# Two-block hybrid layer: first norm's small steps on VectorE, loads of the start reordered, and the small slots kept open through the end of the second block

## The chip, the cores and the metric

One core of a Trainium2 chip runs the whole program. The metric is the device time of one execution in microseconds; the span in a profile runs from the first to the last instruction of the core.

## The reference, cut to what matters

One sequence of 1024 positions and width 1024 passes two blocks, in float32.

```
h = rms_norm(x) @ w_in;  x += [rg_lru(conv(lru_x)) * gelu(lru_gate), sc_b * conv(sc_c * sc_x)] @ w_out
u = conv(rms_norm(x) @ w_up);  x = rms_norm(x + (gelu(gate) * up) @ w_down)        # end of the first block
h = x @ w_in_2  ->  x_q (512), x_kv (256), k_rope (64), gate_a (512), u_pool (512), gate_b (512)
q = rms_norm(x_q) @ w_uq;  k_nope, v = rms_norm(x_kv) @ w_ukv;  rotary parts turned by position
y_a = softmax(causal(q k^T) * scale) v * silu(gate_a)                              # 4 heads
y_b = pool(u_pool, windows 2, 4, 8, 16) * silu(gate_b)
x = layer_norm(alpha * x + [y_a, y_b] @ w_out_2)
```

## The kernel before, in words

Every float32 product is made of three float32r products: an operand is cut into a high part (a cast on ScalarE) and a low part (a subtraction on VectorE), and high x high, high x low and low x high are summed in PSUM. A matmul takes 128 x 128 weights and 512 columns.

**Pairs.** A projection from 1024 inputs is made for two groups of 128 outputs at a time (`Pair`, L229), as seven products of half depth in the manner of Strassen instead of eight. A pair's weight sums are made by loads that accumulate onto a tile in SBUF (`G.dma_start(..., accum_op=ADD)`, L251, L252, L267), issued from GpSimd. `prep_hi` and `prep_lo` (L260, L265) cut an operand, `product` (L269) runs twelve matmuls into one of three PSUM banks of the pair ("x", "y", "z"; the table `GROUP`), and `evac` adds the bank into two result tiles. `Pairs.step` runs one product, keeps the cuts five products ahead and the loads two pairs ahead. The first two pairs of each `Pairs` are interleaved and have `apart` set: their second product has a bank of its own.

**Due times.** `later(d, fn)` puts work off by `d` products; `tick` runs what is due. So the small work of a finished pair (recurrence, convolution, pooling) is spread over the products of the next. The source order sets the priority of the instructions, and a scheduler may change their order on an engine where one is not ready in its model. SyncE (SP) issues the plain loads and stores in one queue, GpSimd (POOL) the accumulating ones and some stores.

**The start.** `start` (L1021) loads x tiles 0 and 1, the gain, x tiles 2 and 3, all pieces of the first two pairs, x tiles 4 to 7, eleven pieces of small vectors (`vec_load`, L148) and the gate weights (`gate_weights_load`, two clears on GpSimd and four loads). `transition` (L472) then norms the eight tiles: `Norm.a` squares and sums (ScalarE), takes the root and the reciprocal (VectorE, L404); `Norm.b` makes five steps on a column of 128 x 1 (GpSimd, L412 to L416) and scales the tile (VectorE, L418); `Norm.T` transposes it on TensorE and cuts it into the moving operands `Hop`.

**The stages.** Fourteen pairs of the mixer with the recurrence (`lru_pair`), its output product (`Rows`), 24 pairs of the feed-forward, its output product, and nine pairs of the second block (`second`, L909): the pooled groups 3 to 0, the low-rank keys and queries, the attention gates. In the middle of these `kr_product` makes the rotary keys.

**End of the second block.** Small tiles of 128 x 1024 float32 come from one pool "u" of `NU` = 23 slots (`U`, L73). After the last pair all due work is drained and the pools are closed and opened anew, the small one with `NU_LATE` = 35 slots, the larger PSUM tiles with two banks each (`PS`). Then come, in this order: `pooled_rows` (fetch pooled rows and weights, L1080; cut, L1133, L1134; product "wob"; row sums with the residual, L1148; store), `q_rope` and `q_nope` for two halves of the heads, `masks_make`, `keys_values`, and attention, in a branch that runs when positions are in order. `head_load` (L1391) fetches the five tiles of the next head (QN, KN, QT) at the second of a head's eight steps; the rotary tiles come by `rot_load`, the turned keys by `keys_rope`.

## Time and profile before

| | us |
|---|---|
| median of 3 runs | 1782.14 |
| lowest and highest | 1781.0, 1783.39 |
| the profiled execution's own time | 1776.74 |
| its span | 1774.6 |

The profile is of one execution, 5.4 us faster than the median. Engines: PE is TensorE's matmuls, PEld its weight loads, DVE is VectorE, ACT ScalarE, POOL GpSimd, SP SyncE. The mean granted TensorE clock of the span is 0.973 of full speed. An engine's idle time is put down to the instruction that, by the profile, ended last among those it waited for; that is inferred, and a wait can bear the name of an instruction that only stood next to the true cause. L110 is the line of every product.

### The profile page before, as it was taken

To read this page: it belongs to the slowest core of one execution; us is meant where nothing else is said; L and a number is where in the kernel's file an instruction comes from. 1 tells how busy PE (TensorE), PEld (TensorE's weight loads), DVE (VectorE), ACT (ScalarE), POOL (GpSimd) and SP (SyncE) were. 2 spreads that over 40 slices of the span, in tenths; PEclk is the share of its full clock that TensorE was granted. 3 is DMA by queue.
4 is the path that set the end of the run, shared out by engine and by line. 5 is a ranking of instruction groups with operands and counts; after the bars stand their busy time and mean duration, and the time that the engine had idled before them with its cause. 6 is when DMAs were issued, how large, how long until landed. Compare 5 with 4: busy or idle time off the path is not lost. (4 is left out here: it accounts for less than half of the span.)

```text
span 1774.6 us, 20249 instructions
## 1 busy us (share of the span) xinstructions
PE 1635.7 (92%) x7347; PEld 1339.8 (75%) x7347; DVE 1191.5 (67%) x1711; ACT 778.3 (44%) x1147; POOL 371.6 (21%) x387
## 2 busy tenths in 40 slices
PE   3898999899998999999999999999999997678997
PEld 3676777678886887887888888888777786557885
DVE  3868666776498797767666754455985755456777
ACT  4566556753064444444444411121653433026761
POOL 4224243211032322222231000010231200020016
PEclk7999999999999999999999999999999998889998
DMA  8556586197156978777774852420586728746232
GB/s 212 103 105 131 105 157 119 30 332 194 14 142 111 191 143 167 150 147 145 160 142 107 306 204 95 101 42 18 150 167 128 149 54 320 217 145 230 99 116 109
DMA packets 272814, 255.36 MB, mean 144 GB/s; under 512 B 18398, under 2 KB 238404, under 8 KB 272708
## 3 DMA queue, kind: packets, MB, share of 16 engines
q1 hardware_dynamic: 168244, 186.80, 32.6%
q0 software_dynamic: 103744, 65.03, 25.4%
q10 hardware_dynamic: 720, 2.18, 0.4%
q8 instruction: 60, 0.98, 0.2%
q14 instruction: 46, 0.38, 0.1%
HBM read 199.56 MB, written 52.82 MB: 142 GB/s over the span
## 5 line engine op out<-in xcount | busy, mean ns | idle before, releaser
L110 PE MATMUL o<-yw 128*128 128x512 f32 x1632 | 375.9, 390 | 0.0
L110 PEld LDWEIGHTS o<-yw 128*128 128x128 f32 x1632 | 305.5, 188 | 63.7 <-DVE yw L530 0.8
L570 DVE TENSOR_TENSOR x<-x,o 128x512 f32<-128x512 f32 x160 | 108.6, 684 | 135.3 <-PE o L110 135.1
L529 ACT CAST yw<-yraw 128x1024 fp32r<-128x1024 f32 x34 | 35.8, 1052 | 193.9 <-PE o L110 172.3
L110 PE MATMUL wob<-yw 128*128 128x512 f32 x192 | 47.0, 408 | 9.0 <-DVE yw L1134 8.9
L402 ACT ACTIVATE xn<-x 128x1024 f32<-128x1024 f32 x24 | 25.6, 1068 | 60.4 <-DVE x L570 54.0
L110 PEld LDWEIGHTS wob<-yw 128*128 128x128 f32 x192 | 37.9, 199 | 18.1 <-ACT yw L1133 9.3
L530 DVE TENSOR_TENSOR yw<-yraw,yw 128x1024 fp32r<-128x1024 f32 x34 | 41.6, 1222 | 14.9 <-ACT yw L529 14.7
L431 PE MATMUL T<-cst,xn 128*128 128x128 f32 x128 | 19.4, 308 | 27.4 <-DVE xn L418 23.1
L530 DVE TENSOR_TENSOR yw<-wraw,yw 128x1024 fp32r<-128x1024 f32 x34 | 41.4, 1218 | 0.4 <-ACT yw L529 0.4
L1459 POOL TENSOR_TENSOR rt<-rt,lng 128x1024 f32<-128x1024 f32 x6 | 14.4, 2403 | 125.3 <-ACT rt L1458 125.3
L431 PEld LDWEIGHTS T<-cst,xn 128*128 128x128 f32 x128 | 17.1, 160 | 30.1 <-DVE xn L418 19.5
L760 DVE TENSOR_TENSOR ffc<-ffc,ffc 128x1024 f32<-128x1024 f32 x24 | 29.4, 1224 | 13.2 <-ACT ffc L757 13.1
L529 ACT CAST yw<-wraw 128x1024 fp32r<-128x1024 f32 x34 | 35.7, 1051 | 3.1 <-DMA wraw<-in_w_down_dram 2.4
L251 POOL DMA_DIRECT2D wu3s<-in_w_in_dram x1 | 1.3, 1282 | 167.9 <-DVE x L570 167.9
L757 ACT ACTIVATE ffc<-ffc 128x1024 f32<-128x1024 f32 x24 | 25.5, 1061 | 24.9 <-DVE ffc L754 24.9
L412 POOL TENSOR_SCALAR ss<-ss 128x1 f32<-128x1 f32 x24 | 7.4, 309 | 132.8 <-ACT ss L403 132.1
L110 PE MATMUL o<-PT,Vh 128*128 128x256 f32 x160 | 30.2, 286 | 4.0 <-DVE PT L1366 3.4
L1345 ACT ACTIVATE sc<-sc,st 128x256 f32<-128x256 f32 (+3 forms) x32 | 26.3, 823 | 15.2 <-DVE st L1344 15.1
L110 PEld LDWEIGHTS o<-PT,Vh 128*128 128x128 f32 x160 | 25.3, 191 | 5.8 <-DVE PT L1366 4.2
L662 POOL TENSOR_TENSOR i<-i,xc 128x1024 f32<-128x1024 f32 x8 | 20.7, 2590 | 42.3 <-ACT i L661 42.3
L437 ACT CAST B<-T 128x512 fp32r<-128x512 f32 x36 | 20.4, 593 | 20.0 <-PE T L431 19.9
(1365 smaller groups left out, 4442.0 us busy)
## 6 DMA issues: line engine op xcount, KB each, us to landing
GY<-ffc SPq DMA_DIRECT2D x24, 512.0 KB
yraw<-GY SPq DMA_DIRECT2D x24, 512.0 KB
wraw<-in_w_down_dram SPq DMA_DIRECT2D x24, 512.0 KB
x<-in_x_dram SPq DMA_DIRECT2D x16, 512.0 KB
yraw<-Y SPq DMA_DIRECT2D x12, 512.0 KB
wraw<-in_w_out_dram SPq DMA_DIRECT2D x12, 512.0 KB
Y<-i SPq DMA_DIRECT2D x8, 512.0 KB
R<-x SPq DMA_DIRECT2D x8, 512.0 KB
```

What stands on the lines that cost most here:

```text
L110: PE.matmul(ps, lhsT=l, rhs=r, start=(first and j == 0), stop=(last and j == n - 1), skip_group_check=not first)
L402: A.activation(xn, X[t], AF.Square, accum_out=ss[:, 0:1])
L431: PE.transpose(ps[:, k * P:(k + 1) * P], src[:, c * P:(c + 1) * P], ident)
L437: A.copy(Hop[m][:, 0, :, sl], src)
L529: A.copy(s[:, j], src)
L530: V.tensor_tensor(s[:, j + 1], src, f(s[:, j]), SUB)
L570: V.tensor_tensor(X[t][:, ns], X[t][:, ns], ps, ADD)
L662: G.tensor_tensor(i, i, st.pop("xc"), MUL)
L757: A.activation(st["g"], st["g"], AF.Gelu_apprx_tanh)
L760: V.tensor_tensor(st["u"], st["u"], st["g"], MUL)
L1345: A.activation(s, s, AF.Exp, scale=QK_SCALE, bias=st[:, 1:2], accum_out=st[:, 2:3])
L1459: G.tensor_tensor(r, r, gB, MUL)
```

## The change

- The first norm's five small steps run on VectorE (`Norm(gB, False, None, V)`); the other norms keep GpSimd.
- The first operand of the first two pairs (`load_first`) is loaded ahead of x tiles 4 to 7, the rest of these pairs behind them; the small vectors and the gate weights are loaded behind the transition.
- The product of number 3 of the first two pairs of every `Pairs` has a bank of its own, no longer the one of number 5; the saved copy of number 5 is added on VectorE after number 6.
- In the recurrence the exponential, its square and the multiplication follow the hyperbolic tangent one tick later, and the rest moves by a tick.
- The rotary key weights are cut at a due time of 14 products and no longer inside `kr_product`. In `second` the pair of pooled group 0 changes place with the first gate pair.
- The pool "u" stays open with 23 slots until the end, and a pool "v" with 12 slots takes the place of the pool "b" for tiles of attention that live long (rotary tiles, turned keys, head 0, masks, first output weights).
- The pooled fetch of groups 3 and 2 and the cut of group 3 stand four products before the end of the pairs; the pooled rows then run in the old pools, with the groups in the order 3, 2, 1, 0, one PSUM bank for each half row, two row sums of half width instead of one, and the first half of the query weights fetched and cut among them. The low-rank keys, the rotary tiles and the second half of the query weights follow after the pools are changed; the masks come behind the last query product.

```
-NU_LATE = 35
+NU_LATE = 12
+    def UV(nm, dt=F32, shape=(P, 1024)):
+        return pools["v"].tile(list(shape), dt, name=f"{nm}_{count[0]}", tag="V", bufs=NU_LATE)
...
+        def load_first(self):
+            if self.a is None:
+                self.a = U(self.nm + "a", F32, (P, 2, 4, P))
+                SY.dma_start(self.a.rearrange("p h k c -> p (h k) c"),
+                             self.ap[:, self.cols[0]:self.cols[0] + P].rearrange("(k p) c -> p k c", p=P))
...
-            new = m in FIRST or m == 2 and self.apart
+            new = m in FIRST or m in (2, 3) and self.apart
...
                 V.tensor_tensor(za[:, n1], (za[:, n1] if 3 in self.seen else zb[:, n0]), ps, SUB)
+                if self.apart:
+                    V.tensor_tensor(za[:, n1], za[:, n1], self.m5, ADD)
...
-            later(10, lru_2)
-            later(11, lru_3)
-            later(12, lru_4)
-            later(13, lru_5)
+            later(9, lru_2)
+            later(10, lru_2b)
+            later(12, lru_3)
+            later(13, lru_4)
+            later(14, lru_5)
...
-                    ga_pair(0), pool_pair(0), ga_pair(2)])
+                    pool_pair(0), ga_pair(0), ga_pair(2)])
...
-        mix.load(2)
+        for p in mix.pairs[:2]:
+            p.load_first()
         for t in range(4, NT):
             X[t] = U(f"x{t}")
             SY.dma_start(X[t], I["x"][0, t * P:(t + 1) * P, :])
-        vec_load()
-        gate_weights_load()
-        norm = Norm(gB, False, None)
+        mix.load(2)
+        norm = Norm(gB, False, None, V)
...
         transition(norm, mix, lambda t: mix.prep(min(max(t - 3, 0), 4)))
+        vec_load()
+        gate_weights_load()
...
-    second.run(lambda: None, lambda: kr_product(kr["raw"]))
-    drain()
-    for nm in ("p", "b", "h", "u"):
-        close_pool(nm)
-    sizes["U"] = NU_LATE
-    open_pool("u")
...
+    later(14, lambda: kr.update(w=split(kr["raw"], "wkr", (P, 8, P))))
...
+    def pooled_begin():
+        pooled_fetch(3)
+        pooled_fetch(2)
+        pooled_cut(3, True)
...
+        pooled_fetch(1)
+        pooled_fetch(0)
+        inv.append(fetch("linv", LINV_d[0]))
...
+        wq["r0"], wq["n0"] = q_rope_load(0), q_nope_load(0)
+        ps = [[PB("wob"), PB("wob")] for _ in range(4)]
+        for e in POOLED:
+            if e < 3:
+                pooled_cut(e)
             for t in range(4):
                 for n in range(2):
-                    products(ps[t][ri], three(y[e], w[e], li, ri), e == 0, True)
+                    products(ps[t][n], terms(e, t, n), e == 3, True)
...
         for t in range(4):
+            rx[t] = fetch("rx", R2_d[t])
+        for t in range(2):
             out(t, ps[t])
         low_norm(LQ, inv[0], 76, "lq")
+        for t in range(2, 4):
+            out(t, ps[t])
+        q_rope_cut(0)
+        q_nope_cut(0)
...
-    pooled_rows()
-    raws = [q_rope_load(0), q_nope_load(0)]
-    q_rope(0, raws[0])
-    raws += [q_rope_load(1), q_nope_load(1)]
+    second.run(pooled_begin, lambda: kr_product(kr["w"]))
+    pooled_rows()
+    for nm in ("p", "b", "h"):
+        close_pool(nm)
+    open_pool("v")
+    open_pool("h")
+    open_pool("p", PSUM)
+    wq["r1"], wq["n1"] = q_rope_load(1), q_nope_load(1)
+    rot_load()
...
+    q_rope(0)
     tick()
-    q_nope(0, raws[1])
-    wkv_raw = [fetch("wkv", w_ukv[k * P:(k + 1) * P, :]) for k in range(2)]
-    q_rope(1, raws[2])
+    q_nope(0)
+    q_rope_cut(1)
+    q_nope_cut(1)
+    wkv = [fetch("wkv", w_ukv[k * P:(k + 1) * P, :]) for k in range(2)]
+    keys_rope()
+    q_rope(1)
+    low_norm(LKV, inv[1], 80, "lkv")
     tick()
+    for k in range(2):
+        wkv[k] = split(wkv[k], "wkv")
+    q_nope(1)
+    LQ.clear()
     masks_make()
-    q_nope(1, raws[3])
-    LQ.clear()
     keys_values()
```

## Rows read from the trace of the kernel before

**Rows 1.** The page's first part: busy time, share of the span and number of instructions of each engine.

```profile
PE 1635.7 (92%) x7347; PEld 1339.8 (75%) x7347; DVE 1191.5 (67%) x1711; ACT 778.3 (44%) x1147; POOL 371.6 (21%) x387
```

**Rows 2.** The table of stretches. Columns: stretch (us from the start of the span), its length, busy us (and instructions) of PE, PEld, DVE, ACT and POOL, granted TensorE clock, busy share of the DMA engines, GB/s moved.

```profile
0.00:26.70 26.70, 6.79 (x37) 6.60 (x37) 2.42 (x11) 6.82 (x14) 11.55 (x30) 0.75 1.05 298
26.70:42.90 16.20, 8.83 (x48) 8.02 (x49) 13.17 (x19) 13.21 (x28) 5.06 (x13) 0.71 0.57 89
1465.30:1474.40 9.10, 0.18 (x2) 0.00 (x1) 1.93 (x3) 3.15 (x3) 0.00 (x0) 0.79 0.85 312
1474.40:1521.50 47.10, 47.03 (x192) 37.87 (x192) 31.20 (x26) 12.61 (x12) 0.00 (x0) 0.93 0.87 307
...
1533.20:1541.60 8.40, 8.39 (x24) 6.30 (x24) 0.68 (x1) 0.00 (x0) 0.00 (x0) 0.66 0.66 201
1465.30:1614.60 149.30, 113.47 (x444) 89.40 (x444) 80.84 (x94) 37.88 (x39) 17.93 (x31) 0.86 0.72 240
```

**Rows 3.** TensorE's waits from 0 to 96 us: who waited for whom, us in total, times, longest.

```profile
PE T L431 <- DVE xn L418: 23.1, 4, 18.8
PE wl L110 <- ACT wl0m L303: 4.7, 1, 4.7
```

**Rows 4.** The order of time from 0 to 75 us, all engines. Columns: start us, duration us, engine, line, operation, tiles written and read, shapes, count, and in brackets the engine's idle time before it and what ended it.

```profile
7.22 0.35 DVE L404 RECIPROCAL ss<-ss 128x1 f32<-128x1 f32 x2 [5.95 <-ACT ss L403]
...
13.26 1.50 POOL L251 DMA_DIRECT2D wl0s<-in_w_in_dram  x1 [12.80 <-DMA wl0s<-in_w_in_dram]
...
19.41 2.79 POOL L613 MEMSET gates<- 128x1024 f32 x2
...
22.31 0.99 POOL L412 TENSOR_SCALAR ss<-ss 128x1 f32<-128x1 f32 x4
...
25.36 3.67 DVE L418 SCALAR_TENSOR_TENSOR xn<-x,ss,g 128x1024 f32<-128x1024 f32 x3 [13.37 <-POOL ss L416]
...
42.91 5.04 PE L110 MATMUL wl<-B,wl0op 128*128 128x512 f32 x12
```

**Rows 5.** TensorE's waits from 1465 to 1615 us: us in total, times, longest.

```profile
PE qr L110 <- ACT wqrh L103: 13.4, 2, 11.7
PE wob L110 <- DVE yw L1134: 8.9, 1, 8.9
```

**Rows 6.** The order of time of TensorE's and SyncE's (SPq) instructions from 1440 to 1545 us, columns as in the fourth group.

```profile
1453.08 8.32 PE L110 MATMUL wga<-T,wga2op 128*128 128x512 f32 x36
...
1467.47 0.34 SPq L1080 DMA_DIRECT2D yb<-YB  x1
...
1526.57 1.47 SPq L1168 DMA_DIRECT2D wqr<-in_w_uq_dram  x2
...
1533.80 0.63 PE L110 MATMUL qr<-lql,wqrh 128*128 128x512 f32 x1
1534.23 0.63 PE L110 MATMUL qr<-lqh,wqrl 128*128 128x512 f32 x1
```

**Rows 7.** The small column tiles "ss" of the norm from 0 to 60 us: count, shortest, median and longest in ns, first and last start.

```profile
L404 DVE RECIPROCAL ss<-ss x8: 154/164/166, 7.2 to 48.6; 128x1 f32<-128x1 f32 x8
...
L413 POOL TENSOR_TENSOR ss<-ss x8: 187/193/715, 23.4 to 48.9; 128x1 f32<-128x1 f32 x8
```

**Rows 8.** The table of stretches again, 5 us each, at the start; columns as in the second group.

```profile
5.00:10.00 5.00, 2.85 (x20) 2.66 (x18) 0.33 (x2) 3.26 (x8) 0.00 (x0) 1.00 1.02 360
10.00:15.00 5.00, 0.00 (x0) 0.00 (x0) 0.33 (x2) 1.61 (x5) 1.74 (x2) 0.82 1.21 298
```

**Rows 9.** DMA issues from 0 to 60 us: count, size of one, median us from issue to landing.

```profile
wl0s<-in_w_in_dram POOLq DMA_DIRECT2D x4, 256.0 KB, 6.4
```

**Rows 10.** The order of time from 1262 to 1300 us (first two pairs of the second block), columns as in the fourth group.

```profile
1276.00 0.62 ACT L260 CAST wu3op<-wu3s 128x512 fp32r<-128x512 f32 x1 [2.09 <-DMA wu3s<-in_w_in_dram]
...
1278.38 0.68 DVE L265 TENSOR_TENSOR wu3op<-wu3s,wu3op 128x512 fp32r<-128x512 f32 x1
...
1279.05 4.61 PE L110 MATMUL wu<-B,wu3op 128*128 128x512 f32 x12 [3.01 <-ACT wu3m L303]
```

**Rows 11.** TensorE's waits from 95 to 365 us (the mixer).

```profile
PE ws L110 <- ACT ws2z L289: 3.1, 1, 3.1
```

**Rows 12.** The order of time from 1330 to 1365 us, around the rotary key product, columns as in the fourth group.

```profile
1344.18 1.14 ACT L260 CAST wqop<-wqs 128x512 fp32r<-128x512 f32 x2 [6.30 <-DMA wqs<-in_w_in_dram]
...
1345.44 0.68 DVE L300 TENSOR_TENSOR wu2z<-wu2z,wu 128x512 f32<-128x512 f32 x1
...
1346.27 4.17 PE L110 MATMUL wu<-B,wu2op 128*128 128x512 f32 x12 [3.45 <-ACT wkrh L103]
```

**Rows 13.** Groups of VectorE's instructions from 1465.3 to 1617 us: line, operation, tiles, shapes, count, busy us, mean ns of one, idle before them and what ended it.

```profile
L1148 DVE SCALAR_TENSOR_TENSOR rx<-rx,wob 128x1024 f32<-128x1024 f32 x8 | 9.8, 1220 | 18.5 <-DMA rx<-Q 11.4 <-PE wob L110 7.0
...
L1280 DVE SCALAR_TENSOR_TENSOR mtmp<-lk,qf,mtmp 128x256 f32<-128x256 f32 x8 | 3.8, 483 | 0.2
```

**Rows 14.** All DMA traffic from 1465.3 to 1614.6 us.

```profile
DMA packets 14971, 35.84 MB, mean 240 GB/s; under 512 B 4571, under 2 KB 6619, under 8 KB 14966
```

**Rows 15.** The chain of work that ended last, one piece: start us, us, what.

```profile
1497.33 5.81 DMA rx<-Q
```

**Rows 16.** SyncE's issues from 1650 to 1710 us, in attention: the fetch for the last head, and of the residual rows for the last product.

```profile
1657.06 0.33 SPq L1395 DMA_DIRECT2D kn<-KN  x1
...
1707.55 0.32 SPq L1424 DMA_DIRECT2D rt<-RR  x1
```

More of the change, by code (lines that the diff above doesn't have):

```diff
@@ L69 @@
     count = [0]
-    sizes = {"U": NU}
     def U(nm, dt=F32, shape=(P, 1024)):
         count[0] += 1
-        return pools["u"].tile(list(shape), dt, name=f"{nm}_{count[0]}", tag="U", bufs=sizes["U"])
+        return pools["u"].tile(list(shape), dt, name=f"{nm}_{count[0]}", tag="U", bufs=NU)
+    def UV(nm, dt=F32, shape=(P, 1024)):
+        count[0] += 1
+        return pools["v"].tile(list(shape), dt, name=f"{nm}_{count[0]}", tag="V", bufs=NU_LATE)
     def HT(nm, dt=F32R, shape=(P, 8, 512)):
@@ L1116, in keys_rope @@
             SY.dma_start(b[32 * r:32 * r + 32, :], KR_d[32 * o:32 * o + 32, :])
-        later(2, lambda: KR.update(w=split(rotate_2(a, b), "kk")))
-    def pooled_rows():
-        y, w, rx = [], [], {}
-        for e in range(4):
-            y.append(fetch("yb", YB_d[e]))
-            w.append(fetch("wob", w_out2[512 + e * P:512 + (e + 1) * P, :]))
-        inv = [fetch("linv", LINV_d[0])]
+        later(2, lambda: KR.update(w=split(rotate_2(a, b), "kk", of=UV)))
+    py, pw, rx, inv, wq = {}, {}, {}, [], {}
@@ new lines, in pooled_fetch, with pooled_cut @@
+    def pooled_fetch(e):
+        assert id(YB_d[e]) in stored
+        py[e] = fetch("yb", YB_d[e])
+        pw[e] = fetch("wob", w_out2[512 + e * P:512 + (e + 1) * P, :])
+    def pooled_cut(e, small=False):
+        if small:
+            py[e], pw[e] = split(py[e], "yb"), split(pw[e], "wob")
+            return
+        s = HT("yw", F32R, (P, 4, 1024))
+        for j, src in ((0, py[e]), (2, pw[e])):
+            A.copy(s[:, j], src)
+            V.tensor_tensor(s[:, j + 1], src, f(s[:, j]), SUB)
+        py[e], pw[e] = (s[:, 0], s[:, 1]), (s[:, 2], s[:, 3])
@@ new lines, with out, terms @@
+    POOLED = (3, 2, 1, 0)
+    def pooled_begin():
+        pooled_fetch(3)
+        pooled_fetch(2)
+        pooled_cut(3, True)
+    def pooled_rows():
+        def out(t, ps):
+            r = rx.pop(t)
+            for n in range(2):
+                ns = slice(n * 512, (n + 1) * 512)
+                V.scalar_tensor_tensor(r[:, ns], r[:, ns], ALPHA, ps[n], MUL, ADD)
+            SY.dma_start(R3_d[t], r)
+        def terms(e, t, n):
+            return three(py[e], pw[e], (slice(None), slice(t * P, (t + 1) * P)),
+                         (slice(None), slice(n * 512, (n + 1) * 512)))
+        pooled_fetch(1)
+        pooled_fetch(0)
+        inv.append(fetch("linv", LINV_d[0]))
+        assert id(LINV_d[0]) in stored
@@ L1156, in pooled_rows @@
-        later(1, rot_load)
-        later(3, keys_rope)
+        for t in range(2, 4):
+            out(t, ps[t])
+        q_rope_cut(0)
+        q_nope_cut(0)
         for t in range(4, NT):
-            p = PS("wob")
-            mm_rows(p, y, w, t)
-            out(t, p)
+            rx[t] = fetch("rx", R2_d[t])
+            ps = [PB("wob"), PB("wob")]
+            for n in range(2):
+                products(ps[n], [x for e in POOLED for x in terms(e, t, n)])
+            out(t, ps)
             tick()
@@ L1196, in q_nope_load, with q_nope @@
         return raw
[L1198 to L1199 removed]
+    def q_nope(p):
+        w = wq.pop(f"n{p}")
         for j in range(2):
@@ L1296, in masks_make @@
         V.tensor_copy(in_order, below[:, 3:4])
-        a, b, c = (U("mask", BF16, (P, 2, S)) for _ in range(3))
+        a, b, c = (UV("mask", BF16, (P, 2, S)) for _ in range(3))
         G.memset(a[:, :, 0:768], 0.0)
@@ L1494 @@
         attention(False)
-    for nm in ("h", "u", "p"):
+    for nm in ("h", "v", "u", "p"):
         close_pool(nm)
```

77 lines of the change are left out of this document (31 added, 46 removed).

## The prediction

> **What bounds the kernel now.** I read the page first: TensorE is busy 92% of the span [rows 1], so time can only come out of the stretches in which it waits or runs at its lower clock. The table of stretches shows where these are [rows 2]. In the first 26.7 us TensorE works 6.79 us, and from 1465.3 to 1614.6, between the last pair of the second block and attention, it is busy 113.47 of 149.3 us at a granted clock of 0.86. The other stages leave little.
>
> For the start I went to TensorE's waits and then to the order of time. It waits 18.8 us for the first normalised tile [rows 3]. VectorE had the first reciprocals at 7.22 us, but the five small steps behind them stand on GpSimd's queue, which first waits until 13.26 for a load that it is to accumulate onto, then clears the gate tiles at 19.41, and comes to the steps at 22.31; the first scaled tile follows at 25.36 and the first product of a pair at 42.91 [rows 4].
>
> For the second block I read the waits of that stretch: 13.4 us (11.7 of it once) for the cut of the rotary query weights and 8.9 us for the first pooled operand [rows 5]. Both are late because their loads are: the pooled fetch is issued at 1467.47, after the pairs have ended, and the query weights at 1526.57, behind all the row stores on SP's queue [rows 6].
>
> **The change, part by part.** *Start.* Forty small steps go from GpSimd to VectorE. One costs 0.19 us on GpSimd, and VectorE's reciprocal of the same column 0.16 us [rows 7]: 40 x 0.16 = 6.4 us more on VectorE, of which five steps (0.8 us) stand ahead of the first tile, so that it can be scaled at about 8 us and not at 25.4, 17 us sooner. GpSimd's queue keeps its accumulating loads and holds nothing up with them. Then the loads decide. Up to the last tile of x there are now 11 transfers of 0.52 MB (x, gain, two first operands), 5.8 MB, at the 298 to 360 GB/s of the crowded windows [rows 8]: 16 to 19 us, so landing at 19 to 22. The six pieces of the two pairs that were loaded before these tiles now follow them (1.6 MB, 4 to 5 us), and a sum lands 6.4 us after its issue [rows 9], at about 30. ScalarE, in order, may have to wait there with tiles still to cut. If nothing of that bites, the start gains 16; if the first product comes no earlier and VectorE's added steps count (it was busy 13.17 of the 16.2 us before that product [rows 2]), it loses 2. I take **-10**, a little above the middle, because the pause that is removed lies ahead of everything else. Eleven small vector loads, two clears and four gate loads move behind the normalisation; they are wanted only when the first pair is complete, so nothing, and 3 us if a slot makes them late.
>
> *Own bank for the fourth product of the first two pairs.* In the second block TensorE waits 3.0 us at that product and the profile names the copy out of its bank [rows 10]. But the operand of the same product was cast only at 1276.00, after ScalarE had waited for its accumulating load, and its low part is done at 1279.06: the product would have stood there anyway. In the mixer the same wait is 4.7 us [rows 3]. The price is six more VectorE adds of 0.68 us [rows 10]. I take **0**, between -4 (the mixer's wait) and +4 (the adds).
>
> *The recurrence's steps spread by one tick.* The same instructions, so no busy time; TensorE's waits on ScalarE's copies, such as 3.1 us once [rows 11], may get shorter: **-1**, between -5 and +3.
>
> *Cut of the key-rotary weights, made earlier.* The wait of 3.45 us in front of that product bears the cut's name, but ScalarE came to it only after 6.30 us of waiting for another pair's load, and VectorE's subtraction at 1345.44, which the product needs, was behind the same [rows 12]: **0**, or -3.5 at best. The swapped order of two pairs: nothing, the same work.
>
> *Second block's end.* The pools of small slots are no longer closed, so the fetch and first cut of the pooled rows stand four products ahead of the end, the fetches of the query operands at its end, and the rotary weights are cut while the pooled product runs. From 1465.3 to the last value product there are 432 matmuls; 36 of them in one run take 8.32 us, (8.32 - 0.39)/35 = 0.227 us each [rows 6], so 98 us is TensorE's own part of the 149.3. Of the other 51 us TensorE is idle for 36 (149.3 less 113.5 [rows 2]); 15 go into matmuls 0.43 us apart, as at 1533.80 and 1534.23 after a pause [rows 6], where the granted clock averages 0.66 [rows 2], between the levels of 1.2 and 2.4 GHz. What is late next? VectorE has 80.84 us there [rows 2], and two half instructions for each row sum cost a little more than the one of 1.22 [rows 13], some 2 us: 83 of 98, no bound but dense. The transfers are nearer: 35.84 MB [rows 14], of which 2 MB move ahead of the stretch; at the 307 to 312 GB/s of its crowded parts [rows 2] the rest takes 109 us, though the next head's loads in it can slip. I take 110 us for the stretch, **-39**, because that bound is the nearest; the ends are 101 (TensorE alone and 3 us of evacuations, -48) and 134 (waits and half clock return to two thirds, -15).
>
> The Trainium skill, page DMA: Bandwidth & Descriptors, section "Anatomy of one DMA — SWDGE (gpsimd) path", puts the moving part of a transfer at bytes over 436 GB/s. By it the 33.8 MB would take an estimated 78 us, under TensorE's 98, and the stretch would be 101; this trace's crowded parts, at 307 to 312 GB/s [rows 2], do not reach that.
>
> *Masks and attention.* The mask steps now come behind the last query product. Eight steps of 0.48 us are the largest of their kind [rows 13]; VectorE may end them after TensorE has ended the values. In attention 23 shared slots and 12 of a second kind replace 35 shared: **+3**, between 0 and +12.
>
> **Sum**: -10 + 0 - 1 + 0 - 39 + 3 = -47. The profiled execution took 1776.74 us, so 1730; the median of the runs, 1782.14, lies 5.4 higher, so **1735**. All best ends give -77, all worst +9, with 3 for late gates. A measurement here can tell about 0.2%, 3.6 us, from no change.
>
> **Rivals.** *TensorE alone bounds the end and the start gains all*: -16 - 1 - 48 + 1 = -64, 1718. For it: VectorE is under 98 us. Against: the transfers' crowding. By the rate on the Trainium skill's page DMA: Bandwidth & Descriptors it would be so.
>
> *The waits come back as others*: 125 us for the stretch, because the row tiles (5.81 us from issue to landing [rows 15]) or VectorE's queue are late where the weights were: -10 - 1 - 24 + 3 = -32, 1750. For it: VectorE already sat waiting 11.4 us for those tiles [rows 13].
>
> *The order of the source is not the order of issue.* GpSimd's clear of the gate tiles stands ahead of the accumulations in the source and ran after them [rows 4]; if the loads come in an order of their own, the start keeps only what the small steps give, -3: -40, 1742.
>
> *Slower: slots.* Where more than 23 of the shared small tiles are alive, a head's five tiles can be fetched only when the former head's last scores have freed theirs. Then three head changes cost a fetch each, 5 x 0.52 MB at the 240 GB/s of the mean [rows 14], 11 us, where the trace fetches them well ahead, at 1657.06; the four last loads, at 1707.55 [rows 16], another 9; and the last four row tiles of the pooled product two landings of 5.81: 33 + 9 + 12 = 54, net +7, 1789. It decides from 19 tiles alive at a head's fetch. I count 16 (five of the current head, four score tiles, one gate, four outputs, two weights) and 21 with the fetch, so it should not bite; later, at the last head, 28 are wanted for a few steps, which is in my +3.
>
> **Chances.** Forecast 0.56 (own range 1720 to 1752), TensorE alone 0.15, waits return 0.17, order of issue 0.05, slots 0.07. The range 1712 to 1766 leaves out the slower case and the far ends. Faster 0.91, same 0.02, slower 0.07.
>
> **What would show it.** Start: first scaled tile near 8 us, first pair product between 26 and 35. Bank: the copy's name gone from TensorE's waits, another in its place. End: pooled product beginning within 1 us of the last pair's, no wait above 3 us for query weights, some 110 us to the first scores, clock near 1. Attention: SP fetching a head's tiles as early as now. I am wrong if the first product stays behind 38 us, or if TensorE still waits over 25 us in that stretch.

## The result, and the profile after

The changed kernel takes 1729.28 us (median of 4 runs, 1726.95 to 1730.28), the kernel before 1781.57 beside it: ratio 0.9703, 95% interval 0.9687 to 0.9720. 1735 was forecast, 1712 to 1766 as the range. The profiled execution took 1726.95, with a span of 1725.2 against 1774.6, so 49.4 us are to be found in the trace.

TensorE's busy time hardly moves [rows 1]; as the span is shorter, its share rises. VectorE has 54 instructions more (the 40 small steps, six adds of number 5, eight more row sums at half width), GpSimd 40 fewer. The page of the profile, first part:

```profile
PE 1627.0 (94%) x7347; PEld 1334.4 (77%) x7347; DVE 1195.2 (69%) x1765; ACT 777.0 (45%) x1147; POOL 359.4 (21%) x347
```

The table of stretches, cut at the landmarks that answer to [rows 2] (first transposes 9.48, first pair product 34.19, last pair's end 1445.4, first scores 1559.4). Columns: stretch, length, busy time of PE, PEld, DVE, ACT, POOL, granted clock, DMA share, GB/s.

```profile
0.00:9.50 9.50, 6.60 (x37) 6.41 (x37) 2.80 (x18) 4.46 (x9) 0.20 (x4) 1.00 0.77 277
9.50:34.20 24.70, 9.03 (x49) 7.42 (x49) 16.98 (x46) 18.07 (x40) 7.98 (x6) 0.63 1.14 255
34.20:95.00 60.80, 57.56 (x254) 46.03 (x253) 56.06 (x109) 33.33 (x57) 16.12 (x13) 0.98 0.70 125
...
1445.00:1488.70 43.70, 43.70 (x194) 36.22 (x193) 24.97 (x29) 9.36 (x10) 0.00 (x0) 1.00 0.68 230
1488.70:1520.00 31.30, 23.14 (x92) 18.19 (x92) 12.65 (x12) 5.35 (x6) 5.21 (x10) 0.84 0.73 210
1520.00:1559.60 39.60, 36.31 (x154) 29.29 (x153) 31.09 (x41) 15.69 (x17) 12.02 (x20) 0.96 0.64 200
1445.00:1559.60 114.60, 103.15 (x437) 83.69 (x436) 68.71 (x81) 30.41 (x33) 17.23 (x30) 0.94 0.68 214
1559.60:1725.00 165.40, 141.11 (x832) 122.78 (x830) 121.08 (x308) 94.52 (x167) 32.55 (x16) 0.94 0.38 137
```

The pooled product (first row of the second group) now runs without a gap. The stretch from the last pair to the first scores is 114.6 us, was 149.3 (147.9 if it too is ended at its first scores, at 1613.2); TensorE stands for 11.4 of it, most between 1488.7 and 1520. From the first scores to the end it is 165.8, was 161.4.

The start in order of time (it answers to [rows 4]; rows of the engines' timelines put in one order):

```profile
8.14 1.28 DVE L428 SCALAR_TENSOR_TENSOR xn<-x,ss,g 128x1024 f32<-128x1024 f32 x1
9.48 1.09 PE L441 MATMUL T<-cst,xn 128*128 128x128 f32 x8 [1.84 <-DVE xn L428]
...
20.45 1.48 POOL L258 DMA_DIRECT2D wl0s<-in_w_in_dram  x1 [20.00 <-DMA wl0s<-in_w_in_dram]
...
25.88 0.62 ACT L267 CAST wl0op<-wl0s 128x512 fp32r<-128x512 f32 x1 [5.25 <-DMA wl0s<-in_w_in_dram]
26.53 0.69 DVE L272 TENSOR_TENSOR wl0op<-wl0s,wl0op 128x512 fp32r<-128x512 f32 x1 [6.01 <-ACT wl0op L267]
...
29.42 1.94 PE L441 MATMUL T<-cst,xn 128*128 128x128 f32 x8 [9.53 <-DVE ss L422]
...
34.19 2.06 PE L112 MATMUL wl<-B,wl0op 128*128 128x512 f32 x4
```

The pause of [rows 4] is gone, and another has come: ScalarE, in order, stands 5.25 us for the accumulated sum of the first pair, VectorE and TensorE behind it. TensorE's waits from 1440 to 1580 (us in total, times, longest), beside [rows 5]:

```profile
PE qr L112 <- ACT wqrh L105: 7.8, 1, 7.8
PE t L1398 <- ACT sc L1388: 6.1, 1, 6.1
PE kn L112 <- DVE knl L106: 3.2, 1, 3.2
```

The wait for the pooled operand (8.9 us) is gone; the one for the query weights is now at the second half of the heads.

### The profile page after: what moved, and what is told of

Its sections match the earlier page's. It is cut to its first block, busy times and chain, and to the rows that moved or that the text cites. A ratio compares the mean times of both kernels' runs of the same rounds, so it can differ in the third digit from the quotient of the medians.

```text
span 1725.2 us, 20241 instructions
## 1 busy us (share of the span) xinstructions
PE 1627.0 (94%) x7347; PEld 1334.4 (77%) x7347; DVE 1195.2 (69%) x1765; ACT 777.0 (45%) x1147; POOL 359.4 (21%) x347
## 5 line engine op out<-in xcount | busy, mean ns | idle before, releaser
L540 DVE TENSOR_TENSOR yw<-yraw,yw 128x1024 fp32r<-128x1024 f32 x34 | 41.5, 1221 | 14.9 <-ACT yw L539 14.8
L112 PE MATMUL wob<-yw 128*128 128x512 f32 x144 | 34.1, 389 | 0.0
L112 PEld LDWEIGHTS wob<-yw 128*128 128x128 f32 x144 | 27.0, 188 | 5.6
L1380 DVE CUSTOM_DVE_ANT_0 sc<-s,mask 128x256 f32<-128x256 f32 (+3 forms) x32 | 25.9, 819 | 6.3 <-PE s L112 5.8
L1398 PE MATMUL t<-cst,sc 128*128 128x128 f32 x160 | 23.3, 277 | 6.6 <-ACT sc L1388 6.1
```

The lines of the kernel that those rows point to most:

```text
L112: PE.matmul(ps, lhsT=l, rhs=r, start=(first and j == 0), stop=(last and j == n - 1), skip_group_check=not first)
L540: V.tensor_tensor(s[:, j + 1], src, f(s[:, j]), SUB)
L1380: V.tensor_tensor_reduce(s, ps[:, 0:w], masks[causal][i][:, 0:w], 1.0, -3.0e38, ADD, MAX, st[:, 0:1])
L1398: PE.transpose(ps[:, k * P:(k + 1) * P], s[:, k * P:(k + 1) * P], ident)
```

## A table of landmarks

The program issues the same products in the same order in all kernels (but for the places named), so the first matmul of a pair is a landmark. Times of the changed kernel's profiled execution in us, and how much later (+) or earlier (-) each other kernel's is there:

| | first pair | mixer's output | 2nd block, first pair | group 2 | group 1 | last gate | first scores | span |
|---|---|---|---|---|---|---|---|---|
| after | 34.2 | 361.6 | 1238.4 | 1309.2 | 1362.1 | 1426.2 | 1559.4 | 1725.2 |
| before | +8.7 | +16.0 | +18.0 | +14.9 | +19.8 | +18.7 | +53.8 | +49.4 |
| v_steps_alone | +1.4 | +4.7 | +7.9 | +6.2 | +12.3 | +11.0 | +45.8 | +41.6 |
| steps_gpsimd | +13.4 | +22.4 | +21.4 | +18.2 | +17.6 | +18.0 | +19.1 | +19.5 |
| loads_old | +1.5 | +7.1 | +5.0 | +2.6 | +2.3 | +2.3 | +3.8 | +4.2 |
| prep_order | -5.0 | +1.1 | +5.0 | +5.2 | +5.0 | +5.1 | +5.8 | +5.8 |
| bank_shared | +0.7 | +4.9 | +12.4 | +10.0 | +10.4 | +10.7 | +10.3 | +10.3 |
| lru_kr_old | -0.5 | +1.2 | +0.8 | -2.5 | +5.7 | +5.7 | +5.6 | +5.6 |
| masks_early | -0.1 | +0.7 | -1.2 | -4.2 | -4.4 | -4.3 | +1.2 | -6.3 |
| q1_cut_early | +0.1 | +3.4 | +2.4 | -0.7 | -1.0 | -1.0 | 0.0 | -0.1 |
| fetch_late | +0.6 | +3.9 | +2.3 | -0.2 | -0.7 | -0.7 | -1.2 | -1.0 |
| queries_late | -0.5 | -0.8 | -2.6 | -5.3 | -5.7 | -5.5 | -5.2 | -5.1 |
| cuts_masks_early | +0.3 | +1.9 | +2.3 | +1.0 | +0.5 | +0.6 | +3.5 | -4.0 |
| groups_forward | +0.5 | +3.1 | +1.8 | -1.2 | -1.5 | -2.8 | +9.4 | +9.8 |

The last six rows are edited only behind group 1's pair. What they differ by ahead of that is the spread between executions: -0.8 to +3.9 at the mixer's output, -2.6 to +2.4 at the second block, -5.3 to +1.0 at its third pair. A difference between two columns of one row is read; one smaller than that spread is not. The executions shown also lie to either side of their kernel's median: queries_late 6.5 us under it, masks_early 3.3 under, bank_shared 5.6 and v_steps_alone 4.5 over.

By the row of before, 16.0 us are won up to the mixer's output, 2.0 in the feed-forward, 0.7 in the second block (3.1 lost, 4.9 won, 1.1 lost), 35.1 from the last gate pair to the first scores, and 4.4 lost behind them: 49.4. In before and groups_forward the six matmuls that pool group 0 (1.4 us) stand behind the landmark of the last gate pair, in the others ahead of it; taken from group 1 on, the end gains 34.0.

## The experiments

Ratios are to the kernel before, five rounds each; the changed kernel's is 0.9703.

| kernel | ratio | 95% interval | median us |
|---|---|---|---|
| v_steps_alone | 0.9911 | 0.9892 to 0.9930 | 1764.10 |
| steps_gpsimd | 0.9794 | 0.9771 to 0.9818 | 1742.45 |
| loads_old | 0.9743 | 0.9724 to 0.9763 | 1733.58 |
| prep_order | 0.9726 | 0.9705 to 0.9746 | 1732.51 |
| bank_shared | 0.9723 | 0.9695 to 0.9752 | 1731.76 |
| lru_kr_old | 0.9724 | 0.9697 to 0.9751 | 1732.03 |
| masks_early | 0.9691 | 0.9662 to 0.9720 | 1724.31 |
| q1_cut_early | 0.9707 | 0.9680 to 0.9733 | 1728.14 |
| fetch_late | 0.9713 | 0.9695 to 0.9731 | 1727.02 |
| queries_late | 0.9716 | 0.9700 to 0.9733 | 1728.41 |
| cuts_masks_early | 0.9675 | 0.9653 to 0.9696 | 1721.58 |
| groups_forward | 0.9770 | 0.9750 to 0.9790 | 1736.79 |

**v_steps_alone**, the kernel before with the small steps on VectorE:

```
-        def b(self, t, N=None):
-            N = N or G
+        E = None
...
+            N = self.E or G
...
+        norm.E = V
```

> The kernel before with one edit: the first norm's five small steps stand on VectorE; loads, banks, ticks and the end stay as they were. Theory (the pause for GpSimd's queue is the larger part of the start, the loads the rest): first scaled tile near 8 us as in the changed kernel, and since the old order of the loads brings the first pair's weight sums sooner (their pieces are issued up to 7.7 us) and x tiles 4 to 7 later (issued 14.7 to 17.3), the first pair product between 33 and 37 us against 42.91: 6 to 10 us faster than before, ratio 0.9945 to 0.9965. Rival (the new order of the loads is what counts): x tiles 4 to 7 hold the cuts up, first product behind 40 us, ratio over 0.998.

Measured: first product at 35.55, 7.4 us earlier than before, as the theory had it, and 11.3 at the mixer's output; ratio 0.9911, so 0.89% of 1780.27, 15.8 us (12.5 to 19.2), where 6 to 10 were expected. (The two executions shown differ by 7.8 at the end: that of before is faster than its kernel's median, this one slower.) The steps alone make most of the start's gain.

**steps_gpsimd**, the changed kernel with the steps back on GpSimd:

```
-        norm = Norm(gB, False, None, V)
+        norm = Norm(gB, False, None)
```

> The changed kernel with its first norm's small steps back on GpSimd, all else kept. On GpSimd's queue four accumulating loads then stand ahead of the first step, and in the changed kernel the first of them waits until 20.0 us for the tile it adds to. Theory (the steps on VectorE are what the start gains): first scaled tile at about 27 us, first pair product at 44 to 47 against 34.19, so 10 to 13 us slower than the changed kernel, ratio to before 0.976 to 0.978. Rival (the start is bound by the loads in either case, the steps beside them cost nothing): first product before 38, ratio within 0.002 of the changed kernel's 0.9703.

TensorE's waits from 0 to 95 us in this kernel:

```profile
PE T L441 <- DVE xn L428: 28.2, 3, 24.2
```

First product at 47.56, 13.4 us later; ratio 0.0091 above the changed kernel's, 16 us. The theory's mechanism, a little over its size. The first product is 4.65 us later than in the kernel before: with the steps on GpSimd the new order of the loads does harm, since the first accumulating load ahead of them on that queue goes out at 21.36 us, not at 13.26, and the first scaled tile comes at 30.01, not at 25.36. The two edits belong together.

**loads_old**, the changed kernel with the old order of the loads at the start:

```
-        for p in mix.pairs[:2]:
-            p.load_first()
+        mix.load(2)
         for t in range(4, NT):
...
-        mix.load(2)
+        vec_load()
+        gate_weights_load()
         norm = Norm(gB, False, None, V)
```

> The changed kernel with the loads of the start in the old order: all pieces of the first two pairs ahead of x tiles 4 to 7, and the small vectors and gate weights ahead of the normalisation. Theory of the prediction (x tiles ahead of the pieces is right, the late loads of the vectors cost nothing): first pair product later than 34.19 by 2 to 6 us, ratio 0.9715 to 0.9740. Rival (in the changed kernel ScalarE stands 5.25 us for the accumulated sum of the first pair, which the old order brings about 6 us sooner): first product at 30 to 34, ratio 0.968 to 0.970.

First product only 1.5 us later, but 7.1 at the mixer's output, of which up to 3.9 can be spread: the theory's direction, with product and ratio just outside its ranges. The ratios differ by 0.0040, and their intervals (to 0.9720, from 0.9724) just do not meet. The order is worth 3 to 7 us, and almost none of it can be seen at the first product.

**prep_order**, the operands of the first two pairs cut in another order:

```
-            self.prep_seq = [(p, m) for m in (1, 5, 2, 6, 3, 7, 4) for p in pairs[:2]]
+            self.prep_seq = [(p, m) for m in (1, 2, 5, 6, 3, 7, 4) for p in pairs[:2]]
```

> The changed kernel with the first two pairs' operands cut in the order 1, 2, 5 instead of 1, 5, 2 (in every set of pairs), so that no cut of an accumulated sum stands among the cuts of the first norm. Theory (ScalarE's and VectorE's stand of 5 to 6 us at 20 to 26 us, both for the accumulated sum, delays the transposes behind it and with them the first product): that stand is gone, first pair product at 28 to 31 against 34.19, 3 to 6 us faster than the changed kernel, ratio 0.967 to 0.969; in the other two sets of pairs no difference over 1 us each. Rival (the fifth product, which needs the sum, waits instead): first product early but TensorE waits as long before product 5, ratio within 0.001 of 0.9703.

The stand for the sum is gone and the first product starts at 29.16, 5.0 us earlier. At the mixer's second lru pair (80.3 us in the changed kernel) the lead is 1.0, and the whole is not faster. So the theory held for the first product and failed for the time. The lead goes within the first two pairs:

```profile
43.49 0.62 ACT L267 CAST wl0op<-wl0s 128x512 fp32r<-128x512 f32 x1 [4.37 <-DMA wl0s<-in_w_in_dram]
...
45.69 0.51 PE L112 MATMUL wl<-T,wl0op 128*128 128x512 f32 x1 [1.74 <-ACT T L447]
```

ScalarE stands 4.37 us for the next accumulated sum instead, TensorE waits behind it, and its matmuls run slower: the first twelve of a pair take 4.85 us at a granted clock of 0.50 (4.14 at 0.68 in the changed kernel), and eleven behind the wait 4.39. That is the rival's way, at another product than it named. What is left of the lead is hidden by chance: TensorE waits 3.9 us at the mixer's third lru pair here, 0.7 in the changed kernel, but 3.4 in q1_cut_early, whose code is the same there.

**bank_shared**, product 3 back in product 5's bank:

```
-            new = m in FIRST or m in (2, 3) and self.apart
+            new = m in FIRST or m == 2 and self.apart
...
-                if self.apart:
-                    V.tensor_tensor(za[:, n1], za[:, n1], self.m5, ADD)
```

> The changed kernel without the own bank for product 3 of the first two pairs: it again adds into product 5's bank, and the extra add on VectorE is gone. Theory of the prediction (the operand of that product stands late anyway, the bank is worth 0 within -4 to +4): the copy out of the bank is named again in TensorE's waits, once or twice with 3 to 5 us, but the product after it starts within 1.5 us of where it does now; from the second block's first pair to its third (in the changed kernel 1238.4 to 1309.2) up to 3 us less, since before had 3.1 us less there; ratio 0.968 to 0.972. Rival (the bank removes a true wait of TensorE): the 4.7 us of the mixer and the 3.0 us of the second block come back, product output of the mixer 4 to 5 us later, ratio 0.973 to 0.975.

In the feed-forward, 500 to 580 us, TensorE waits

```profile
PE wf L112 <- DVE wf1z L304: 3.8, 1, 3.8
PE wf L112 <- ACT wf0m L310: 2.6, 1, 2.6
```

and in the second block, 1235 to 1400,

```profile
PE wu L112 <- ACT wu3m L310: 3.2, 1, 3.2
```

The copy's name is back, as in [rows 10]. In the second block it costs nothing (from its first pair to group 2 it takes 2.4 us less than the changed kernel's execution, but so do most kernels with the own bank: -3.3 to +0.2): there the operand is late anyway. In the mixer it is +4.9, but only +1.4 behind the first two pairs, and 3.8 us of wait stand at the third lru pair, where kernels of the same code have 0.4 to 3.5. In the feed-forward it is +7.5, where the six kernels of the spread have -1.9 to +0.4; before and v_steps_alone, which share the bank too, wait there for the same two results and have +2.0 and +3.2. The ratio is 0.0020 up, 3.6 us, with intervals that overlap. So a gain of some 2 to 7 us by the profile, in the feed-forward, which the times do not settle.

**lru_kr_old**, the recurrence's old ticks and the key-rotary cut inside its product:

```
-            later(9, lru_2)
-            later(10, lru_2b)
-            later(12, lru_3)
...
+            later(10, lru_2)
+            later(11, lru_3)
...
-        w = raw
+        w = split(raw, "wkr", (P, 8, P))
```

> The changed kernel with two small parts undone: the recurrence's steps on their old ticks, and the key-rotary weights cut inside their product again. Both lie in different stages, so that each is read from where the pairs begin. Theory of the prediction: recurrence -1 (the mixer, from its third lru pair to the output product, 1 us longer when undone), kr 0 (the product waits for ScalarE's queue, which waits for another pair's load); ratio 0.970 to 0.972. Rival (the kr cut is a wait of its own: between the pairs of pooled group 2 and pooled group 1 the changed kernel gained some 5 us on before): those pairs 4 to 6 us further apart than the 52.9 us of the changed kernel, ratio 0.973 to 0.974.

The recurrence: +1.2 at the mixer's output, inside the spread. The cut: from group 2 to group 1 the pairs lie 8.2 us further apart. The rows there, by time:

```profile
1329.09 1.14 ACT L267 CAST wqop<-wqs 128x512 fp32r<-128x512 f32 x2 [8.07 <-DMA wqs<-in_w_in_dram]
1329.74 1.29 DVE L272 TENSOR_TENSOR wqop<-wqs,wqop 128x512 fp32r<-128x512 f32 x2 [6.86 <-ACT wqop L267]
1330.13 1.04 ACT L105 CAST wkrh<-wkr 128x1024 fp32r<-128x1024 f32 x1
1330.95 0.68 DVE L309 TENSOR_TENSOR wu2z<-wu2z,wu 128x512 f32<-128x512 f32 x1
1331.77 5.07 PE L112 MATMUL wu<-B,wu2op 128*128 128x512 f32 x12 [5.82 <-DVE wu2z L309]
1336.68 0.63 PE L112 MATMUL kr<-B,wkrh 128*128 128x512 f32 x2
```

and in the changed kernel:

```profile
1325.57 0.69 DVE L309 TENSOR_TENSOR wu2z<-wu2z,wu 128x512 f32<-128x512 f32 x1
1328.42 2.88 PE L112 MATMUL wu<-B,wu2op 128*128 128x512 f32 x12
1329.42 1.14 ACT L267 CAST wqop<-wqs 128x512 fp32r<-128x512 f32 x2 [5.28 <-DMA wqs<-in_w_in_dram]
1330.07 1.29 DVE L272 TENSOR_TENSOR wqop<-wqs,wqop 128x512 fp32r<-128x512 f32 x2 [3.81 <-ACT wqop L267]
```

The wait does not stand at the key-rotary product but ahead of the last product of group 2's pair, number 3. It adds into the bank of number 5 (the bank that the change parts for the first two pairs alone), so the add on VectorE that reads number 5 (L309) has to come first. ScalarE waits for the load of wqs in both kernels. With the cut inside its product, L309 stands on VectorE's queue behind the low parts of wqs and is late with them; with the cut made early it stands ahead of them, TensorE goes on, and the key-rotary product fills the time until the next pair's operands are cut. The 8.2 us are the wait of 5.8 and twelve matmuls of 5.07 us (granted clock 0.53) instead of 2.88. The order of L309 goes with the place of the cut in all fourteen kernels: behind in lru_kr_old, before and v_steps_alone, ahead in the eleven others. Neither L309 nor the cut of wqs was edited; why their order on the queue changed is not shown.

**masks_early**, the masks ahead of the last query product:

```
     tick()
+    masks_make()
     for k in range(2):
         wkv[k] = split(wkv[k], "wkv")
     q_nope(1)
     LQ.clear()
-    masks_make()
```

> The changed kernel with the mask steps ahead of the last query product, as before, instead of behind it. In the changed kernel VectorE makes masks until 1566.6 us, 7 us after the first scores, and TensorE waits 6.08 us for the first exponentials and goes on at half clock. Theory (the loss of attention, 4.4 us from the first scores to the end, comes from the late masks alone): first scores no later than now by over 1 us, from them to the end 161 to 163 us against 165.8, ratio 0.968 to 0.970. Rival (VectorE is dense before attention, so what it does earlier delays the keys and values by as much; or the loss lies in the shared slots): first scores later by 3 to 5 us, or the stretch behind them still 165 to 166, ratio 0.970 to 0.972.

TensorE's waits, 1440 to 1580:

```profile
PE qr L112 <- ACT wqrh L105: 7.8, 1, 7.8
PE kn L112 <- DVE wkvl L106: 7.2, 1, 7.2
PE t L1398 <- ACT sc L1388: 1.4, 2, 0.9
```

From the first scores to the end 158.4 us, 7.4 less than the changed kernel and 3.0 less than before: the loss of attention was the late masks and no slots. From the last gate pair to the scores it gives 5.5 back, as the rival said: the wait is now for the cut of the key weights, behind the masks on VectorE. The ratio, 0.9691, is not told from 0.9703.

**q1_cut_early**, the second rotary query weights cut earlier:

```
     q_rope(0)
+    q_rope_cut(1)
     tick()
     q_nope(0)
-    q_rope_cut(1)
     q_nope_cut(1)
```

> The changed kernel with the second rotary query weights cut right behind the first rotary product, ahead of the first plain query product, instead of behind it. In the changed kernel their cast stands on ScalarE behind the turned first queries, which wait for a transfer and VectorE, and TensorE waits 7.8 us at that product. Theory (the wait is one of order on ScalarE's queue, not of the load): that wait falls under 1 us and the first scores come 6 to 8 us earlier, ratio 0.966 to 0.968. Rival (VectorE's queue is dense, the wait moves to the keys): the wait at the keys, 3.2 us now, grows to 8 to 10, first scores within 2 us of now, ratio 0.969 to 0.971.

TensorE's waits, 1440 to 1580:

```profile
PE qn L112 <- ACT wqnh L105: 6.5, 1, 6.5
PE t L1398 <- ACT sc L1388: 6.0, 1, 6.0
PE kn L112 <- DVE knl L106: 3.9, 1, 3.9
```

The wait left the rotary product and stands at the next one, whose cut is still behind the same turned queries on ScalarE. First scores 0.0: neither theory had the place, the rival had the time.

**cuts_masks_early**, both cuts ahead of the first rotary product, and the masks between the key weights' cut and the last query product:

```
+    q_rope_cut(1)
+    q_nope_cut(1)
     q_rope(0)
...
     for k in range(2):
         wkv[k] = split(wkv[k], "wkv")
+    masks_make()
     q_nope(1)
```

> The changed kernel with two steps moved: both cuts of the second query weights ahead of the first rotary product, and the masks behind the cut of the key and value weights, ahead of the last query product. Theory (the waits of 7.8 and 6.1 us are of order on ScalarE's and VectorE's queues; VectorE has 11 us of idle time around 1490 and 4 us behind it, so the work fits): no wait over 3 us at the second query products, 3 to 6 at the keys, from the first pooled product to the first scores 106 to 112 us against 114.1, from there to the end 158 to 162 against 165.8; together 8 to 14 us faster than the changed kernel, ratio 0.962 to 0.966. Rival (before attention VectorE's queue is the bound: what moves forward moves the keys back): stretch to the scores 114 to 120, then 158 to 162, ratio 0.967 to 0.970.

TensorE's waits, 1440 to 1585:

```profile
PE kn L112 <- DVE ends L1331: 12.1, 1, 12.1
PE t L1398 <- ACT sc L1388: 1.4, 2, 0.9
PE kn L112 <- DVE wkvl L106: 1.3, 1, 1.3
```

The waits at the queries are gone, and 12.1 us stand at the keys, behind the mask steps. First pooled product to first scores 117.1 against 114.1, then 158.3 against 165.8: the rival in both. Still it is the fastest kernel of all here, ratio 0.9675 (0.9653 to 0.9696), 5 us under the changed kernel by ratio, with intervals that overlap a little.

**fetch_late**, the pooled fetch and first cut behind the last pair:

```
-    second.run(pooled_begin, lambda: kr_product(kr["w"]))
+    second.run(lambda: None, lambda: kr_product(kr["w"]))
+    drain()
+    pooled_begin()
```

> The changed kernel with the fetch of the first two pooled groups and the cut of the first one behind the last pair, not four products ahead of its end; the pools stay as in the changed kernel. Theory of the prediction (the first pooled operand was late because its load was): from the last pair's product to the first pooled one TensorE waits for a landing of some 5.8 us and a cut of 2.3, so 8 to 12 us come back before the pooled product, and as nothing behind it has slack on TensorE they stay: stretch from the first pooled product to the first scores as now, 114, ratio 0.975 to 0.977. Rival (the stretch is bound by transfers and by VectorE and ScalarE's queues, which use the pause): of the 8 to 12 us the waits behind, 11 us now, give back more than half, ratio 0.971 to 0.973.

Neither: no change at all, -0.7 at the last gate pair and -1.2 at the first scores. SP's queue issues the first fetch at the same place as before the edit:

```profile
1413.50 0.34 SPq L1089 DMA_DIRECT2D yb<-YB  x1
...
1434.73 2.90 SPq L1089 DMA_DIRECT2D lq<-LQ  x4
```

(1414.23 in the changed kernel, 1434.38 for the first lq.) By the profile this fetch waits on SP's queue in both kernels for a slot, which a cut of the last gate pair's weights frees (SP's waits from 1380 to 1490, the same row in both):

```profile
SPq L1089 <- DVE wga2op L272: 38.8, 2, 35.4
```

SP had nothing else to do meanwhile, so here a later line in the source is no later issue.

**queries_late**, the first query weights fetched and cut behind the last pooled row:

```
-        wq["r0"], wq["n0"] = q_rope_load(0), q_nope_load(0)
...
-        q_rope_cut(0)
-        q_nope_cut(0)
...
     pooled_rows()
+    wq["r0"], wq["n0"] = q_rope_load(0), q_nope_load(0)
+    q_rope_cut(0)
+    q_nope_cut(0)
```

> The changed kernel with the first half of the query weights fetched and cut behind the last pooled row, not at the start of the pooled product. Theory of the prediction (the 11.7 us wait before was one of a late load): the loads are issued behind the last row tiles, the wait at the first rotary product is 8 to 13 us, ratio 0.975 to 0.978. Rival (the slots come free early enough: in the changed kernel the second half's loads are issued at 1480 to 1487, two to eight us before the first rotary product): wait of 3 to 6 us there, and the second half's 7.8 us wait grows by no more than 3, ratio 0.972 to 0.975.

The load moved by 30 us (1469.51 against 1439.60), and TensorE's times did not:

```profile
1469.51 0.45 SPq L1196 DMA_DIRECT2D wqr<-in_w_uq_dram  x1
```

From the last gate pair to the first scores +0.3; the wait for the second half is 7.8 as now. It still stands 13.7 us ahead of its product (1483.21), where before it was issued 6.6 ahead of it [rows 6]. It is not the place of before either: there all eight row stores stand ahead of it on SP's queue, here five.

**groups_forward**, the groups and the pairs in the old order:

```
-                    pool_pair(0), ga_pair(0), ga_pair(2)])
+                    ga_pair(0), pool_pair(0), ga_pair(2)])
...
-    POOLED = (3, 2, 1, 0)
+    POOLED = (0, 1, 2, 3)
...
-        pooled_fetch(3)
-        pooled_fetch(2)
-        pooled_cut(3, True)
+        pooled_fetch(0)
+        pooled_fetch(1)
+        pooled_cut(0, True)
...
-    second.run(pooled_begin, lambda: kr_product(kr["w"]))
+    second.run(lambda: None, lambda: kr_product(kr["w"]))
+    drain()
+    pooled_begin()
```

> The changed kernel with the pooled groups in the order of before: the pairs of pooled group 0 and of the first gate change back their places, the pooled product takes the groups 0, 1, 2, 3, and the fetch of groups 0 and 1 stands behind the last pair (a place that alone changed nothing). The pools stay open as in the changed kernel. In the trace of before SP's queue stands empty from about 1400 to 1467.47, 67.1 us of it put down to the store of group 0's rows, which the first fetch reads; in the changed kernel that store is issued at 1424.71 and its fetch comes last of the four, at 1431.99. Theory (the order of the groups is what let the fetches and all the loads behind them on SP's queue go ahead, not the open pools and not the place in the source): the first fetch comes within 4 us of the last pair's end again, TensorE waits 8 to 11 us for the first pooled operand, the loads of queries and row tiles are late by 30 us and more, and 10 to 25 us of the 35 come back, ratio 0.976 to 0.984. Rival (the prediction's: open pools and the early fetch): as the pools are open, at most the 3 to 5 us of one late store, ratio 0.971 to 0.974.

What SP's queue waits for in the kernel before, from 1400 to 1490:

```profile
SPq L1080 <- DMA YB<-wu0z: 67.1, 1, 67.1
```

and here, from 1380 to 1585, with the first fetch and the wait of TensorE that follows:

```profile
SPq L1089 <- DMA YB<-wu0z: 68.4, 1, 68.4
```

```profile
1445.93 0.34 SPq L1089 DMA_DIRECT2D yb<-YB  x1
...
1456.93 1.62 SPq L1199 DMA_DIRECT2D wqr<-in_w_uq_dram  x2
```

```profile
PE wob L112 <- ACT wobh L105: 8.9, 1, 8.9
PE qr L112 <- ACT wqrh L105: 7.7, 1, 7.7
```

The wait of 8.9 us for the first pooled operand [rows 5] is back, though the pools stay open: from the last gate pair to the first scores 12.2 us more, of which 1.4 are the pooling matmuls that changed sides of that landmark; from group 1 on 10.9, and by the ratio (0.0067 up) 12. The theory, but for its "30 us and more": the loads of the queries are 17 us late, those of the row tiles 13. With group 0 first and its pair late, the first load on SP's queue reads what the last-but-one pair stores, and every load behind it stands too.

## Why the prediction came out, point by point

- **Start, -10.** Right in mechanism, too small: 16.0 us at the mixer's output (with the bank and the ticks there), where -16 was the best end. The first scaled tile at 8.14 and the first product at 34.19 are as said, and ScalarE's stand for a sum is the one I feared. The error is in the yardstick: the first product moved 8.7 us, and 7.3 more came between it and the output, which the runs v_steps_alone (7.4, then 11.3) and loads_old (1.5, then 7.1) show too. All of the 7.3 lies in the first two pairs: from the first product to the second lru pair 46.1 us, 53.4 before, for the same 190 matmuls; TensorE stands 3.2 of them against 8.0, and the matmuls take 42.9 at a granted clock of 0.97 against 45.4 at 0.93. The 8.0 hold the 4.7 us wait of [rows 3], but bank_shared gives only 0.7 back there; the rest was not taken apart.
- **Own bank, 0.** Right in the second block and for the reason given; too small in the feed-forward, where three kernels with the shared bank wait 2.2 to 3.8 and 2.3 to 2.7 us for its two results and lose 2.0 to 7.5. By the ratios 3.6 us, which is within their uncertainty.
- **Recurrence, -1.** Not told from nothing.
- **Cut of the key-rotary weights, 0.** Wrong. The wait for the load on ScalarE did stay, as argued; the step that failed is that VectorE's subtraction "was behind the same". It was so in the kernel before (the wait of 3.45 us stands ahead of group 2's last product, not of the key-rotary one), but with the cut made early that step goes ahead of the late load's cuts. In the trace of before the pairs are 5.0 us further apart, undone 8.2.
- **The swapped pairs: "nothing, the same work".** Wrong, and the costliest line of the reading. With the groups' order it is 11 of the 34 us from group 1 to the first scores, 12 by the ratio. I put the late fetch down to the closed pools and the place in the source; fetch_late shows that the place is worth nothing with the new order and open pools, groups_forward that with open pools the fetch is late all the same. The trace of before names the store among SP's own waits (67.1 us), which the prediction left out. What the new order would bring with the pools closed was not run.
- **The second block's end, -39 to 110.** 114.6 and -35.1. The size held, the bound did not: the DMA queues moved 214 GB/s over the stretch, 24.5 MB, not 33.8, because 7.6 MB (13 tiles of 0.52 and the first query weights) were issued ahead of it, and heads' tiles came later. What holds the 114.6 above the 98 of the matmuls are 11.4 us of waits of order, on ScalarE's queue at the second query weights and on VectorE's at the keys, and matmuls at the lower clock behind them (0.84 from 1488.7 to 1520). That is the rival "waits come back as others" in kind, 4.6 us over the forecast where it had 15. Two of the signs named failed with it: no wait over 3 us for query weights (7.8), clock near 1 (0.94). By the rate of the Trainium skill, page DMA: Bandwidth & Descriptors, section "Anatomy of one DMA — SWDGE (gpsimd) path" (it is on transfers issued from GpSimd, here 8.1 of the 24.5 MB), the transfers would bind nothing and the stretch be 101; that their rate binds nothing agrees, but the stretch is 13.6 longer, by order on the queues (in it VectorE waits 2.4 us once for a small transfer, the turned first queries).
- **The other 23 us of the stretch.** groups_forward keeps them against before: 13.6 from the start of the pooled product to the first rotary product (11.7 of them the wait in front of that product, [rows 5]), 5.9 in the first rotary product, 6.5 from there to the keys, 3.1 lost behind. Which of half-row banks, loads ahead of the row stores, and later loads of the keys does it, no run undid alone; that stays open.
- **Masks and attention, +3.** 4.4, and the reason holds: masks_early wins it back and 3.0 more.
- **Slots.** Did not bite: the last head's tiles are fetched 48.4 us behind the first scores, 43.9 before, with attention itself slower by 4.4, and masks_early is faster in attention than the 35 slots of before.

By the landmarks the mixer with its start gained 5 us more than the sum has (16.0 for 11), the feed-forward 2 and the key-rotary stage 5 more; the end fell short by 4, attention by 1, and the second block lost 4 elsewhere, so the sum of -47 met 49.4. That errors of this size cancel is luck. The other 3 us between 1735 and 1729.28 are the executions shown: that of before lay 5.4 under its median, that of the changed kernel 2.3.

## What to carry to other kernels

Before costing a late load, ask what its own queue waits for: one fetch that reads a late store, issued first, holds every independent load behind it, and what is fetched first then matters more than where the fetch is written. Of a wait that bears a cut's name, ask which product stands behind it and what that product needs: here it was an add on VectorE, and its place on the queue moved with a cut that it does not read. Read the gain of a start at a landmark well behind it, not at the first product.

## What the runs showed of the hardware

The same code differs by -5.3 to +3.9 us at the landmarks from execution to execution. One place where it does so: at the mixer's third lru pair TensorE waits 0.7 us in one execution and 3.4 in another, where ScalarE waits 4.0 us for an accumulating load in the second and 0.4 in the first (after, q1_cut_early). A run that undoes 3 us needs a landmark next to it.

In the start single microseconds carry over 400 GB/s, near the 436 of the Trainium skill's page DMA: Bandwidth & Descriptors (same section), above the 298 to 360 that I took from windows of 5 us; but while the accumulating loads run (issued from 20.45 on) it falls to 157 to 183; from 24 to 31 us all but 5 of the 2316 packets are theirs. Mean GB/s in 40 slices of 1 us from 0 to 40 in the changed kernel:

```profile
GB/s 0 53 283 373 397 254 258 385 422 375 330 290 299 360 410 414 406 410 338 297 289 291 291 257 183 177 159 176 164 157 137 105 25 124 116 34 297 196 0 117
```
